# A two-layer transformer kernel: PSUM layout kept through the MLP, last MLP chunk computed plainly in token groups, adaLN dot products moved among the up projections

## The chip, the cores and the metric

The kernel runs on one core of one Trainium2 chip. The metric is device time in microseconds (us): the median of several executions. The engines are PE (TensorE, matrix multiplication), DVE (VectorE), ACT (ScalarE), POOL (GpSimd) and SP (SyncE, which here only issues transfers). PSUM, where PE leaves its products, has eight banks; a bank holds 512 fp32 values in each of 128 partitions.

## What is computed

Two layers over 512 latent tokens and 256 context tokens, model width 1024, MLP width 4096. Only the MLP and the modulation concern the change:

```python
def sq_relu_mlp(h, w1, w2):
    return jnp.square(jax.nn.relu(h @ w1)) @ w2
...
    for l in range(DEPTH):
        last = l == DEPTH - 1
        mod_x = (jax.nn.silu(c) @ w_ada[l] + b_ada[l])[:, None, :]
        mod_c = jax.nn.silu(c_ctx) @ w_ada[l] + b_ada[l]
...
        x = x + g1 * ox
        x = x + g2 * sq_relu_mlp(modulate(rmsnorm(x, norm_mlp[l]), sh2, sc2), w_ff1[l], w_ff2[l])
        if not last:
            h = h + cg1 * oc
            h = h + cg2 * sq_relu_mlp(modulate(rmsnorm(h, norm_mlp[l]), csh2, csc2), w_ff1[l], w_ff2[l])
    return rmsnorm(x, norm_final)
```

In layer 0 both streams go through the MLP (768 tokens, side by side as columns), in layer 1 only the latent one (512).

## The kernel before

Activations lie with features on partitions and tokens as columns. Every fp32 operand of a large product is split into a high and a low part (ACT copies the high part, L208; DVE subtracts it to get the low one, L217), and a product is three matmuls (`mm3`, all recorded on L200). Weights come in units by transfers from SP's queue (`load_unit`, L225 and L233) into four raw buffers, and are split in pieces of up to 512 columns, four pieces ahead of the task that needs them (`emit`, AP_ = 4). The work is a list of tasks. `merge` interleaves two lists by the costs written into the tasks; a scheduler then orders each engine's instructions, mostly in the order of the tasks, and later ones that are ready may go ahead.

The MLP (`layer_ff`) runs over chunks of the MLP width: 8 chunks in layer 0, 4 in layer 1. A chunk has an up projection (4 or 8 output tiles, one unit `w_ff1` each; relu and square on ACT, L1366 and L1367) and a down projection (2 or 4 blocks, one unit `w_ff2` each). The down projection multiplies 2 x 2 block matrices with seven products instead of eight: the tokens are cut into two halves (384 or 256 columns), the features into even and odd tiles. For this DVE forms sums of weight quarters (`quarter`, L244: S1 to S4) and of activations (`evac`: T1 to T4, L1357 and L1369), and what the seven products give is added in two ways. `gate` (L1418) adds a product times the modulation to the residual `x`; `keep` (L1357, in the first chunk a copy by ACT, L1426) adds it to one of three running sums U, 5, 7, which `finish` combines in the last chunk and passes through `gate`. Each product of the seven goes into a PSUM tile of one bank; `begin` opens a pool of eight such tiles for the MLP (`self.psum(0, 8)`), where the rest of the kernel has tiles of two banks (`A`) and of one bank (`B`).

In the last chunk the last two blocks (in layer 0 both) run five products first and then S1 and S4, with the norm of the first token half laid among these. `push` and `stat_push` (L514, L518) add the squares of `x` for the norm, `stat_end` sums them over partitions with a matmul (`ssum`), `rstd` (L528 to L532) makes the factor and `norm_h` (L545 to L549) the next input `h`. The norm of the second half follows everything. In layer 1 the final norm and the stores take the place of `norm_h` (`final_tasks`).

The output projection ahead of the MLP (`residual_tasks`, tiles `res`) ends in another form: its last four output tiles (TAIL0 = 4) run once for each of three token groups (0 to 255, 256 to 511, 512 to 767), and the norm of one group is laid among the products of the next.

The modulation vectors of layer 1 are dot products on DVE (`ada_rows_tasks`, L468): a task loads a piece of 128 rows by 512 columns of the transposed weight into one of three buffers (`rows`, N_RR = 3) and multiplies it with `silu(c)` and, for the first 32 of 96 tasks, also with `silu(c_ctx)`. Each is kept behind the last marked instruction of the MLP on DVE (`issue_after(self.mark.ins)`). In the emission they are merged among all tasks of layer 0's MLP but the first 4 and the last 40 (`ff[4:FT]`). Chunk 0's up projection also holds the adaLN work of layer 0 for two other vectors (`ff1`: 4 tasks of matmuls, 8 of double rows).

## Time and profile before

| | |
|---|---|
| median of 3 runs | 1646.73 us (1646.69 to 1647.88) |
| the profiled execution, its time | 1643.82 us |
| its span (first to last instruction) | 1642.0 us |
| MLP of layer 0, first matmul to the next layer's first | 418.4 to 992.5 us |
| MLP of layer 1, first matmul to the end | 1269.8 to 1642.0 us |

Times in the trace are microseconds from the span's start. PE is matmuls, PEld the loads of weights into the array, which overlap them. PEclk is the granted TensorE clock as a share of 2.4 GHz, a mean over the stretch. An idle time has what ended it behind "<-". A row "x120" of a timeline merges so many instructions that followed one another.

### The profile page before, as it was taken

How to read it: one execution, taken by the hardware profiler on the slowest of the kernel's cores; microseconds unless marked ns; L12 is line 12 of the kernel's file. 1: busy time of each engine (PE TensorE's matmuls, PEld its weight loads, DVE VectorE, ACT ScalarE, POOL GpSimd, SP SyncE). 2: the span in 40 equal slices, each digit the busy share in tenths (PEclk: the TensorE clock that was granted, in tenths of full speed). 3: DMA queues.
4: the chain of work that ended last, by engine and by line, in shares of the span. 5: the costliest groups of instructions: out<-in, count | busy, mean ns of one | idle time of the engine just before them, and what ended most of it. 6: DMA issues, size and time to landing. Idle time of an engine off the chain costs nothing.

```text
span 1642.0 us, 26299 instructions
## 1 busy us (share of the span) xinstructions
PE 1533.6 (93%) x9840; PEld 1375.8 (84%) x9840; DVE 1245.5 (76%) x2761; ACT 830.4 (51%) x1746; POOL 38.0 (2%) x78
## 2 busy tenths in 40 slices
PE   4999999998999999999999848999998999999995
PEld 2898567877799999999999737967887999999995
DVE  5665756877786988988979896677646785969688
ACT  4425467554445344344353334367754656464653
POOL 0010000000000000000000000101000000000000
PEclk8999999999899999999999968999999999999997
DMA  9352545553242413334345133524323232232311
GB/s 371 113 151 65 144 107 126 185 171 117 84 134 71 142 61 113 120 106 148 119 132 167 53 117 102 179 69 110 100 85 115 78 110 97 83 125 78 123 58 52
DMA packets 69103, 192.08 MB, mean 117 GB/s; under 512 B 8944, under 2 KB 11504, under 8 KB 68976
## 3 DMA queue, kind: packets, MB, share of 16 engines
q1 hardware_dynamic: 65584, 180.18, 34.1%
q0 software_dynamic: 2816, 9.70, 2.6%
q8 instruction: 77, 1.26, 0.3%
q10 hardware_dynamic: 576, 0.52, 0.1%
q14 instruction: 50, 0.41, 0.1%
HBM read 159.97 MB, written 10.49 MB: 104 GB/s over the span
## 4 chain that ended last, share of the span: by engine, by line
PE 76%; DVE 18%; ACT 2%; DMA 2%; issue 1%; SPq 0%; DVEq 0%; ACTq 0%
PE f L200 40%; PE A L200 10%; PE sc L200 4%; DVE x L1418 3%; PE oe L200 3%; DVE wt L217 3%; PE pv L200 3%; PE res L200 3%; DVE V L1357 3%; PE pT L1025 2%; PE rv L200 2%; DVE sum L244 2%; PE ada L200 2%; DVE rows L468 1%; PE ro L200 1%
## 5 line engine op out<-in xcount | busy, mean ns | idle before, releaser
L200 PEld LDWEIGHTS f<-h,wt 128*128 128x128 f32 x3120 | 451.6, 190 | 5.6 <-issue 3.8
L200 PE MATMUL f<-h,wt 128*128 128x256 f32 (+1 forms) x3120 | 454.1, 308 | 1.2 <-DVE nv L528 1.0
L200 PE MATMUL f<-act,wt 128*128 128x384 f32 (+1 forms) x2688 | 419.7, 316 | 19.7 <-DVE x L1418 10.4
L200 PEld LDWEIGHTS f<-act,wt 128*128 128x128 f32 x2688 | 401.6, 193 | 35.9 <-ACT wt L208 12.8
L217 DVE TENSOR_TENSOR wt<-raw,wt 128x512 fp32r<-128x512 f32 (+1 forms) x320 | 218.8, 689 | 88.1 <-ACT wt L208 85.6
L208 ACT ACTIVATE wt<-raw 128x512 fp32r<-128x512 f32 (+1 forms) x320 | 195.0, 626 | 165.4 <-PE f L200 64.0
L200 PE MATMUL A<-h,wt 128*128 128x512 f32 (+2 forms) x864 | 172.5, 358 | 1.8 <-DVE nv L528 1.3
L200 PEld LDWEIGHTS A<-h,wt 128*128 128x128 f32 x864 | 144.4, 192 | 28.3 <-DVE nv L528 2.4
L208 ACT ACTIVATE wt<-sum 128x512 fp32r<-128x512 f32 x128 | 77.5, 629 | 173.5 <-DVE sum L244 165.1
L1366 ACT ACTIVATE b<-f 128x384 f32<-128x384 f32 (+1 forms) x130 | 55.6, 430 | 125.2 <-PE f L200 125.2
L217 DVE TENSOR_TENSOR wt<-sum,wt 128x512 fp32r<-128x512 f32 x128 | 86.8, 689 | 12.0 <-ACT wt L208 10.7
L1418 DVE SCALAR_TENSOR_TENSOR x<-f,mod,x 128x256 f32<-128x256 f32 (+2 forms) x186 | 88.5, 501 | 1.4 <-PE f L200 1.0
L200 PE MATMUL sc<-k,q 96*128 96x512 f32 (+1 forms) x384 | 85.6, 350 | 2.6 <-ACT p L1007 2.0
L468 DVE SCALAR_TENSOR_TENSOR rows<-rows,sbc 128x512 f32<-128x512 f32 x128 | 86.5, 687 | 0.4
L208 ACT ACTIVATE act<-T 128x384 fp32r<-128x384 f32 (+1 forms) x128 | 58.9, 472 | 53.5 <-DVE T L1369 29.6
L200 PEld LDWEIGHTS sc<-k,q 96*128 96x128 f32 x384 | 62.8, 188 | 20.4 <-issue 5.5
L1357 DVE TENSOR_TENSOR V<-V,f 128x384 f32<-128x384 f32 (+1 forms) x162 | 79.3, 511 | 0.1
L217 DVE TENSOR_TENSOR act<-b,act 128x384 fp32r<-128x384 f32 (+1 forms) x96 | 46.8, 489 | 42.8 <-ACT act L208 42.7
L1006 DVE TENSOR_REDUCE st<-sc 128x1 f32<-128x768 f32 x64 | 60.7, 953 | 15.6 <-PE sc L200 15.2
L217 DVE TENSOR_TENSOR act<-T,act 128x384 fp32r<-128x384 f32 (+1 forms) x128 | 60.5, 487 | 12.4 <-ACT act L208 11.4
L1026 ACT ACTIVATE pT<-pT 128x384 f32<-128x384 f32 x128 | 56.5, 491 | 22.9 <-PE pT L1025 22.4
L200 PE MATMUL res<-mix,wt 128*128 128x256 f32 (+1 forms) x384 | 58.8, 312 | 2.3 <-DVE om L1046 1.9
(243 smaller groups left out, 1893.2 us busy)
## 6 DMA issues: line engine op xcount, KB each, us to landing
raw<-w_ff SPq DMA_DIRECT2D x128, 512.0 KB, 3.7
rows<-w_adaT SPq DMA_DIRECT2D x128, 256.0 KB, 2.8
raw<-w_in SPq DMA_DIRECT2D x22, 512.0 KB, 3.9
raw<-w_ada SPq DMA_DIRECT2D x16, 512.0 KB, 10.9
rows<-w_ada SPq DMA_DIRECT2D x32, 256.0 KB, 3.2
raw<-w_out SPq DMA_DIRECT2D x16, 512.0 KB, 3.6
x<-xd SPq DMA_DIRECT2D x6, 768.0 KB, 7.2
x<-xT SPq DMA_DIRECT2D x4, 768.0 KB, 6.8
```

What stands on the lines that cost most here:

```text
L200: self.nc.tensor.matmul(out, l, r, start=start, stop=stop)
L208: self.nc.scalar.activation(out, src, AF.Copy, **k)
L217: return self.nc.vector.tensor_tensor(out, src, hi.bitcast(F32), op=ALU.subtract)
L244: self.nc.vector.tensor_tensor(t, a, b, op=ALU.add)
L468: nc.vector.scalar_tensor_tensor(out, w, 1.0, self.sbc[:, v, half], op0=ALU.mult, op1=ALU.mult, accum_out=acc[:, v, i, j:j + 1])
L1006: nc.vector.tensor_reduce(st[:, 0:1], ps, axis=AX, op=ALU.max, negate=True)
L1025: nc.tensor.transpose(ps[:, kt, :], p[:, (k0 + kt) * P:(k0 + kt + 1) * P], self.ident)
L1026: nc.scalar.activation(s["pT", h, qt // 2][:, k0:k0 + 3, c], ps, AF.Copy)
L1357: add = lambda x, y, z, op=ALU.add: nc.vector.tensor_tensor(x, y, z, op=op)
L1366: nc.scalar.activation(b[:, at:at + n], ps, AF.Relu)
L1418: self.mark = nc.vector.scalar_tensor_tensor(x, ps[:, at - o:at - o + n], g[:, cond:cond + 1], x, op0=ALU.mult, op1=ALU.add)
```

## The change

`begin` no longer changes the PSUM pools: three tiles of two banks and two of one bank stay through the MLP. In layer 0 the two halves of an up tile, and the two output tiles of one of the seven products, share a two-bank tile; `keep` then handles both at once, 768 columns wide. In layer 1 `bank` hands out the two halves of such a tile one after the other, and an up tile is one product of 512 columns.

The last chunk is computed plainly, with eight products and neither sums of weights nor of activations (`split_plain`, `plain`). All blocks but the last take all tokens at once, the last one runs once for each token group, and the norm of a group is laid among the products of the next (`late`). `finish` moves into the last chunk's up projection, merged with its tasks. The norm's parts follow the token groups instead of the halves.

The dot products of layer 1's modulation are handed to `layer_ff`, which merges a share (14 of 96 tasks, at the end 13) into the up projection of each chunk but the last. In chunk 0 they follow the tasks of `ff1` in one list.

```diff
-            self.psum(0, 8)
...
+    def bank(self, name):
+
+        if self.half is None:
+            self.half = self.A(name, (P, 2, 512))
+            return self.half[:, 0, :]
+        t, self.half = self.half, None
+        return t[:, 1, :]
...
-        then = self.final_tasks(groups) if last else self.norm_tasks(l + 1, self.G1, 0, halves)
+        then = self.final_tasks(groups) if last else self.norm_tasks(l + 1, self.G1, 0, groups)
...
+        def split_plain(c, m, half):
...
+            f = act[c, m]
+            s = slice(0, w) if half is None else slice(half * hw, half * hw + hw)
+            b = st["b", m % 2][:, s]
+            self.hi(f[:, 0, s], b)
+            self.mark = self.lo(f[:, 1, s], b, f[:, 0, s])
...
         def up(c, m, u):
+            if last:
+                ps = self.bank("f1")
+                self.lin1(ps, u, H, NK, 0, w)
+                evac(c, m, None, [(ps, 0, w)])
+                return
+            ps = self.A("f1", (P, 2, 512))
...
-        def keep(c, j, name, ps):
-            v = st[name][j]
-            if c == 0 and (name, j) not in st:
-                st[name, j] = True
+        def keep(c, blk, name, ps):
+            v = st[name, "all"][:, MP * blk:MP * blk + MP]
+            if c == 0 and (name, blk) not in st:
+                st[name, blk] = True
                 nc.scalar.activation(v, ps, AF.Copy)
             else:
                 self.mark = add(v, v, ps)
...
-        def product(c, u, i, j, name, then=None):
+        def product(c, u, blk, name):
             q, f = use[name]
-            ps = self.B([P, hw], "f2")
+            ps = self.bank("f2")[:, None, :hw] if last else self.A("f2", (P, 2, 512))[:, :, :hw]
             t = u.pieces[name].t
-            for p in range(CP):
-                s = slice((i * CP + p) * P, (i * CP + p + 1) * P)
-                self.mm3(ps, t[:, 0, s], t[:, 1, s], *part(c, p, q), p == 0, p == CP - 1)
-            (then or f)(c, j, ps)
+            for i in range(MP):
+                for p in range(CP):
+                    s = slice((i * CP + p) * P, (i * CP + p + 1) * P)
+                    self.mm3(ps[:, i, :], t[:, 0, s], t[:, 1, s], *part(c, p, q), p == 0, p == CP - 1)
+            f(c, blk, ps)
...
+        def plain(c, u, blk, i, odd, gs):
+
+            ps = self.A("f2")
+            m = 2 * (MP * blk + i) + odd
+            for o, n, _ in gs:
+                for side, name in enumerate((A21, A22) if odd else (A11, A12)):
+                    t = u.pieces[name].t
+                    for p in range(CP):
+                        s = slice((i * CP + p) * P, (i * CP + p + 1) * P)
+                        f = act[c, 2 * p + side]
+                        self.mm3(ps[:, o:o + n], t[:, 0, s], t[:, 1, s], f[:, 0, o:o + n], f[:, 1, o:o + n],
+                                 side == p == 0, side == 1 and p == CP - 1)
+            for o, n, cond in gs:
+                self.gate_update(l, m, ps, 5, o, n, cond)
+                self.stat_push(m, o, n)
...
+        spread = self.extra.pop(("ff", l), [])
         for c in range(n_chunk):
...
+            if c == n_chunk - 1:
+                ups = merge(ups, [Task(1, lambda j=j: finish(j)) for j in range(4)])
+            extra = self.extra.pop(("ff1", l), []) if c == 0 else []
+            share = -(-len(spread) // max(n_chunk - 1 - c, 1))
+            extra, spread = extra + spread[:share], spread[share:]
+            out += merge(ups, extra)
             blocks = [Unit(a["w_ff2"][l, c * n_blk + blk], 2048, "st") for blk in range(n_blk)]
...
+            if c < n_chunk - 1:
+                for blk in range(n_blk):
+                    out += block(c, blk, blocks[blk])
+        out.append(Task(0, self.stat_start))
+        for blk in range(n_blk - 1):
+            out += plain_tasks(c, blocks[blk], blk, whole)
+        late = []
+        for i, g in enumerate(groups):
+            ts = plain_tasks(c, blocks[-1], n_blk - 1, [g])
+            for j, t in enumerate(ts):
+                out.append(t)
+                share = -(-len(late) // (len(ts) - j))
+                out += late[:share]
+                late = late[share:]
+            late = list(then[i])
+        return out + late
...
-            tasks += e.pop(("mid", l), []) + merge(ff[:4], e.pop(("ff1", l), [])) + merge(ff[4:FT], e.pop(("ff", l), [])) + ff[FT:]
+            tasks += ff
```

## Rows read from the trace of the kernel before

**Rows 1.** The page, part 1: busy us (share of the span) and instructions by engine

```profile
PE 1533.6 (93%) x9840; PEld 1375.8 (84%) x9840; DVE 1245.5 (76%) x2761; ACT 830.4 (51%) x1746; POOL 38.0 (2%) x78
```

**Rows 2.** Windows: stretch, length, busy us of PE, PEld, DVE, ACT, POOL, PEclk, DMA

```profile
418.40:460.30 41.90, 39.60 (x262) 36.16 (x261) 29.48 (x70) 19.75 (x46) 0.00 (x0) 0.97 0.33 108
...
524.40:557.00 32.60, 31.04 (x170) 28.82 (x169) 31.36 (x70) 11.54 (x21) 0.00 (x0) 1.00 0.29 96
557.00:590.20 33.20, 33.20 (x194) 33.20 (x193) 25.85 (x59) 15.93 (x31) 0.00 (x0) 1.00 0.32 105
...
851.80:883.70 31.90, 30.75 (x170) 28.89 (x170) 30.63 (x68) 11.54 (x21) 0.00 (x0) 1.00 0.40 123
...
917.00:950.00 33.00, 24.94 (x127) 24.01 (x126) 31.99 (x71) 8.55 (x17) 0.00 (x0) 0.84 0.19 65
...
971.50:992.50 21.00, 2.90 (x4) 1.18 (x4) 17.59 (x39) 9.18 (x19) 0.00 (x0) 0.55 0.52 189
...
1402.20:1442.00 39.80, 39.80 (x338) 39.80 (x337) 38.47 (x79) 18.89 (x35) 0.00 (x0) 1.00 0.34 109
```

**Rows 3.** PE timeline, layer 0's last down projection: start, us, engine, line, what, [idle before]

```profile
916.95 19.55 PE L200 MATMUL f<-act,wt 128*128 128x384 f32 x108
944.44 6.82 PE L200 MATMUL f<-act,wt 128*128 128x384 f32 x24 [7.94 <-DVE x L1418]
960.61 1.65 PE L200 MATMUL ssum<-ss,one 128*128 128x384 f32 x2 [9.35 <-DVE ss L518]
...
988.39 1.62 PE L200 MATMUL ssum<-ss,one 128*128 128x384 f32 x2 [17.08 <-DVE ss L518]
...
992.55 7.75 PE L200 MATMUL A<-h,wt 128*128 128x384 f32 x30 [1.26 <-DVE nv L528]
```

**Rows 4.** PE timeline, layer 0's output projection up to the MLP

```profile
368.31 24.09 PE L200 MATMUL res<-mix,wt 128*128 128x512 f32 x156 [0.93 <-DVE om L1046]
...
411.41 1.22 PE L200 MATMUL ssum<-ss,one 128*128 128x256 f32 x2 [6.25 <-DVE ss L518]
413.50 1.22 PE L200 MATMUL ssum<-sq,one 128*128 128x256 f32 x2 [0.87 <-ACT sq L514]
416.50 1.92 PE L200 MATMUL ada<-rows,sc 128*32 128x512 f32 x4 [1.78 <-DVE nv L528]
```

**Rows 5.** PE timeline, layer 1's MLP: an up projection, and its last down projection

```profile
1356.62 45.73 PE L200 MATMUL f<-h,wt 128*128 128x256 f32 x384
...
1573.07 15.82 PE L200 MATMUL f<-act,wt 128*128 128x256 f32 x132
...
1624.44 6.61 PE L200 MATMUL f<-act,wt 128*128 128x256 f32 x36
```

**Rows 6.** PE timeline, layer 1's input projection: 48 matmuls of 512 columns

```profile
1012.39 11.50 PE L200 MATMUL A<-h,wt 128*128 128x512 f32 x48 [0.43 <-ACT rx L698]
```

**Rows 7.** Groups by line and form: xcount | busy, mean ns of one | idle before

```profile
L217 DVE TENSOR_TENSOR wt<-sum,wt 128x512 fp32r<-128x512 f32 x128 | 86.8, 689 | 12.0 <-ACT wt L208 10.7
...
L1357 DVE TENSOR_TENSOR V<-V,f 128x384 f32<-128x384 f32 x112 | 59.1, 553 | 0.0
...
L531 DVE SCALAR_TENSOR_TENSOR nq<-nv,nq 128x768 f32<-128x768 f32 x5 | 4.8, 955 | 3.2 <-ACT nq L530 3.2
```

**Rows 8.** Windows of the dot products alone (L468): stretch, length, DVE busy, PEclk, DMA

```profile
524.40:557.00 32.60, 5.62 (x16) 1.00 0.29 96
557.00:590.20 33.20, 7.00 (x20) 1.00 0.32 105
```

**Rows 9.** DVE timeline, chunk 0's up projection: the fourth and fifth row in succession

```profile
450.76 0.68 DVE L468 SCALAR_TENSOR_TENSOR dot<-rows,sbc 128x512 f32<-128x512 f32 x1
...
453.48 0.69 DVE L468 SCALAR_TENSOR_TENSOR dot<-rows,sbc 128x512 f32<-128x512 f32 x1 [1.30 <-DMA rows<-w_adaT]
```

**Rows 10.** DVE timeline, chunk 1's down projection: the second gate of the first product

```profile
532.81 0.61 DVE L1418 SCALAR_TENSOR_TENSOR x<-f,mod,x 128x384 f32<-128x384 f32 x1
```

More of the change, by code (lines that the diff above doesn't have):

```diff
@@ L53 @@
 TAIL1 = 2
-FT = -40
 TL = False
@@ L158, in __init__ @@
         self.dp = pool("dp", N_DP)
-        self.ps = None
+        self.ps = self.half = None
         self.es = es
```

115 lines of the change are left out of this document (54 added, 61 removed).

## The prediction

> **What bounds the kernel now.** I read the page's busy times first, then the windows by stage, then the PE timeline of the stages that came out too long, then the DVE's work in them. Over the span PE is busy 93% and DVE 76% [rows 1], but the MLP of each layer has stretches with other limits [rows 2]. In layer 0 an up projection of one chunk (192 matmuls) takes 33.2 us with PE busy throughout, 173 to 174 ns a matmul. A down projection has 168 of them, so 29.3 us if nothing holds it; the six of chunks 1 to 6 (the first is 524.40 to 557.00, the last 851.80 to 883.70) take 192.8 us together, 32.1 each, and DVE is busy for 31 of those 32. So DVE holds PE for 2.8 us in each, 17 us in all. In the up projection the same DVE has 7 us to spare.
>
> The dear place is the last chunk of layer 0. Its down projection starts at 916.95 and the next layer's first matmul at 992.55 [rows 3]: 75.6 us for the same 168 matmuls. PE waits 7.94 us for a gate, 9.35 us for the sum of squares, 17.08 us for the second one; DVE is busy for 32.0 of 33.0 us at the start of it, and the granted clock sinks to 0.55 at the end [rows 2]. Layer 1 has the same ending, smaller: its last down projection runs from 1573.07 to 1631.05, 58.0 us [rows 5], where the others take 39.8 [rows 2]. Its other stages have no gap on PE at all.
>
> **Term 1, the last chunk of layer 0.** The seven products become eight plain ones: 4 output tiles over (512, 256) columns and 4 in three groups of 256, that is 48 matmuls of 512 and 144 of 256, with the norm of a group laid among the products of the next. The kernel has this very form already, at the end of the output projection of the same layer (residual_tasks with TAIL0 = 4: the same tiles, the same three groups, 12 matmuls a product, the same norm_tasks). So I take its time rather than add one up: from its first matmul at 368.31 to the moment PE is free for the next stage at 416.50 (the adaLN matmuls there have no counterpart) are 48.2 us, of which 6.25 + 0.87 + 1.78 are waits [rows 4]. 48.2 - 75.6 = **-27.4 us**. DVE has less to do than before: no weight sums, 4 split pieces a block in place of 7 (689 ns each [rows 7]), no activation sums, no dot products. The four `finish` steps move into the up projection of that chunk, which has no dot products any more; DVE was busy there for some 19 us without them (below), so they are hidden. Without that cover they would lie on the path with up to 16 us: 4 times 8 instructions of about 0.5 us each (an addition takes 0.55 [rows 7]). Bounds: -33, if the waits of 9 us go too, and -15, if half of the present waits stay.
>
> **Term 2, layer 1.** Its last down projection becomes 144 matmuls of 512 and 96 of 256. A matmul of 256 goes at 45.73 / 384 = 119.1 ns [rows 5]; one of 512 at 11.50 / 48 = 239.6 ns at most [rows 6]. 144 x 0.2396 + 96 x 0.1191 = 45.9 us in place of 58.0: **-12.1 us**. The two norms around it are as they were. The up projection turns 48 matmuls of 256 into 24 of 512 a tile: 238.2 against 239.6 ns or a little under it, so I take 0 (bounds +1 and -4 us over 720 pairs). In the other down projections DVE is busy 38.5 of 39.8 us [rows 2] and now has six banks in pairs rather than eight single ones to be late in: 0, with +5 as the bound. Bounds of the term: -17 and -6.
>
> **Term 3, chunks 0 to 6 of layer 0.** All 128 dot products of layer 1's adaLN leave the down projections; a share of 14 rows goes into each up projection. The first 32 rows carry two dot products each. Ten dot products took 7.00 us in one up projection [rows 8], 0.70 each, and without them DVE was busy for 25.85 - 7.00 = 18.9 us there [rows 2]. So:
> - Chunks 3 to 6: 18.9 + 14 x 0.70 = 28.7 us in 33.2: hidden. Chunk 2 (4 double rows): 31.5, just hidden.
> - Chunk 1: 18.9 + 28 x 0.70 = 38.5 in 33.2, 5 us too much. It also has the last rows behind the last tile, ahead of the first product's evacuation. +4 us after what its down projection loses now (3.3).
> - Chunk 0: it also keeps the 8 double rows and 4 matmul tasks that it has now. 29.5 [rows 2] + 19.6 = 49.1 us in a window of 41.9. 7 us too much, and the rows behind the first two tiles can't use the time in which DVE waits for them: +8 us (0 to 20).
>
> In the down projections DVE falls to 31.4 - 5.6 = 25.8 us [rows 2, 8], and a wide `keep` costs at most 955 ns where two narrow ones cost 1106 [rows 7], another 1 us a chunk. But the PSUM turns get shorter. The release of the first product's pair of banks is the gate that ends at 533.4, 9.0 us after the down projection began at 524.4 [rows 2, 10]. With eight single banks PE runs 8 products ahead (8 x 6 x 174 ns = 8.4 us); with three two-bank tiles it has three pairs, 6.3 us. The products ahead of that gate are the same afterwards (activation splits, then the last rows). So I expect a wait of 2.7 us in each, before the fourth pair, in place of 2.8 spread out: 0 for chunks 2 to 6. Behind it the unloaded DVE catches up. Term 3: **+12 us**, bounds -17 (all present waits go) and +25. The row loads go past nothing new: they stay in SP's queue among the weights, in front of which they wait for a dot product to free one of three buffers.
>
> **Sum.** -27.4 - 12.1 + 12 = -27.5 us. The profiled execution has a span of 1642.0 and a time of 1643.82; the median shown is 1646.73, 2.9 more. The span becomes 1614.5, the median about 1619.
>
> **Rivals.** (A) *The up projection swallows the dot products.* PE needs the late activations only from the third product on, and DVE had idle time in chunk 0. Then term 3 is about -15 and the time 1592. For it: DVE's total per chunk (18.9 + 25.8 + 9.8) is below PE's 62.5 us. Against it: the double rows lie in the first two chunks, where it isn't.
>
> (B) *Three PSUM tiles hold PE all through the down projections*, not once: a second wait like the first, 3 us in seven of them, 1640. The Trainium skill ("Perfetto Trace Analysis", Optimization Strategy) warns of just this: a gap that repeats on the engine that should be saturated can mean that there is no PSUM for the next tile, by buffer count or tile size. By that rule the change goes the wrong way. The rows of before show PE held in these stages even with eight banks, which agrees; they also show DVE full at the time, so which of the two it was they can't tell. Further, the skill ("TensorE: Matmul & The Clock Gate", A second HAM failure mode: psum-queue depth-cycling) reports a clock that oscillates when PE stops briefly between PSUM turns. In the rows of before the granted clock stayed at 1.00 in the down projections that lost 2.6 to 3.3 us, and fell to 0.84 and 0.55 only with waits of 8 to 17 us, so I give it nothing of its own.
>
> (C) *Slower: the rows are paced by their three buffers.* Place: the up projections of chunks 0 to 6. Dot products are in order on DVE, and one that waits for its row holds the splits of the next tile's activations and weights behind it. Behind three rows in a row the next came 2.72 us after the one before it, with 1.30 us of waiting for the transfer [rows 9]. At that pace 14 rows take 38.1 us, 4.8 too long, in six chunks 29 us, and chunk 0 with some 17 rows behind its first two tiles 46 us where there are about 22: +24. With terms 1 and 2 that is +13.5: 1660. It decides from 33.3 / 14 = 2.4 us a row on. Against it: three loads in flight make it about (3 + 1.4) / 3 = 1.5 us, and the rows come in threes with 8 us between.
>
> (D) *The tail doesn't become like the output projection's*: DVE comes late into it, and term 1 is -13: 1633. The change not doing what it says can't be seen in the code; every part has its place in the order.
>
> **Chances.** Forecast 0.60 (own range 1607 to 1631), A 0.15, B 0.09, C 0.07, D 0.09. A measurement of this kernel can tell about 0.2%, 3.3 us. Faster: the forecast, A, B, D but for their ends, 0.91; within: 0.03; slower: C, 0.06. The range leaves out most of C and the far half of A: 1594 to 1642.
>
> **What would show it.** After the change: from the start of layer 0's last down projection to the next layer's first matmul 48 us (over 60 is D); layer 1's last down projection 46 us; in chunk 0 a wait of some 8 us on PE around the first down projection for an activation split or a gate, in chunk 1 some 7; in chunks 2 to 6 one wait of 2 to 3 us before the fourth pair, with DVE as releaser (many of them is B, none is A); up projections of 33 us in which DVE waits little for rows (many waits for the row transfers are C). It would be wrong above all by how late DVE comes out of the first two up projections.

## The result, and the profile after

The changed kernel takes 1657.07 us (median of 4 runs, 1655.85 to 1657.78), the kernel before beside it 1646.82 us (1646.69 to 1647.88): a ratio of 1.006, interval 1.0043 to 1.0077. It is slower by 10 us where 28 us of gain were forecast. The spans of the profiled executions are 1655.8 and 1642.0 us.

PE is busier by 19 us although it executes 740 matmuls fewer than before ([rows 1] against part 1 of the page after):

```profile
PE 1552.9 (94%) x9100; PEld 1351.4 (82%) x9100; DVE 1183.5 (71%) x2564; ACT 802.4 (48%) x1635; POOL 38.2 (2%) x78
```

The plain last chunk works. These are PE rows of the changed kernel from layer 0's last down projection to the next layer's first matmul (the matmuls A); they answer [rows 3]. The columns are start, us, engine, line, operation, count and, in brackets, the idle time before the row with what ended it.

```profile
966.47 23.62 PE L206 MATMUL f<-act,wt 128*128 128x512 f32 x153
...
990.60 5.98 PE L206 MATMUL f<-act,wt 128*128 128x256 f32 x48
996.86 1.44 PE L206 MATMUL f<-act,wt 128*128 128x256 f32 x10 [0.28 <-DVE x L1243]
...
1009.03 1.22 PE L206 MATMUL ssum<-ss,one 128*128 128x256 f32 x2 [6.21 <-DVE ss L524]
1010.71 0.98 PE L206 MATMUL A<-h,wt 128*128 128x384 f32 x2 [0.46 <-ACT h L554]
```

From 966.47 (three matmuls of the projection stand earlier, at 961.44) to 1010.71 are 44.2 us, where 916.95 to 992.55 were 75.6. The waits of 7.94, 9.35 and 17.08 us have become one of 6.21 us, the one that the output projection's tail had before [rows 4].

The first chunks went the other way. Windows of chunks 0, 1 and 2 after (stretch, length, busy us of PE, PEld, DVE, ACT, POOL, PEclk, DMA share, GB/s), to be held against 72.7 us for chunk 0 before (418.4 to 491.1) and 65.8 for chunk 1 (to 556.9):

```profile
405.40:512.00 106.60, 86.49 (x437) 73.55 (x438) 85.95 (x214) 40.80 (x82) 0.00 (x0) 0.86 0.37 115
512.00:587.90 75.90, 68.02 (x362) 65.01 (x361) 63.51 (x145) 27.74 (x52) 0.00 (x0) 0.93 0.32 102
587.90:657.20 69.30, 64.48 (x362) 61.99 (x361) 56.42 (x123) 27.84 (x52) 0.00 (x0) 1.00 0.36 113
```

Chunk 0 starts 13 us earlier than before (405.39 in place of 418.43) and ends 21 us later. Among its PE rows stand these waits, and below them the ACT row that the longest one hangs on:

```profile
446.31 1.91 PE L206 MATMUL ada<-rows,sc 128*32 128x512 f32 x2 [2.33 <-DMA rows<-w_ada]
...
471.31 6.97 PE L206 MATMUL f<-h,wt 128*128 128x384 f32 x24 [7.03 <-ACT b L1409]
...
488.21 23.92 PE L206 MATMUL f<-act,wt 128*128 128x384 f32 x120 [3.42 <-ACT wt L214]
```

```profile
470.77 0.49 ACT L1409 ACTIVATE b<-f 128x384 f32<-128x384 f32 x1 [8.79 <-DVE dot L474]
```

PE waits 7.03 us for ACT to read an up tile; ACT, idle for 8.79 us, waits for a dot product. Why it must, the experiments show.

A middle chunk of layer 0 after, from 726.12 to the next at 794.46 (chunks 3 to 6 are alike, 68.3 to 68.9 us, where all but chunk 0 had 65 to 66 before). PE first:

```profile
726.12 29.60 PE L206 MATMUL f<-h,wt 128*128 128x384 f32 x168
755.55 2.07 PE L206 MATMUL f<-act,wt 128*128 128x384 f32 x11
757.46 4.32 PE L206 MATMUL f<-h,wt 128*128 128x384 f32 x24
761.62 4.50 PE L206 MATMUL f<-act,wt 128*128 128x384 f32 x25
769.91 24.72 PE L206 MATMUL f<-act,wt 128*128 128x384 f32 x132 [3.79 <-DVE x L1453]
```

Two things are new. The second half of the last up tile (x24) comes behind the first 11 matmuls of the down projection, and after 36 matmuls, which is three pairs of products, PE waits 3.79 us for the gate of the first pair. DVE before that gate (the wide `keep`, the last two dots of the chunk, the two gates):

```profile
762.00 0.95 DVE L1363 TENSOR_TENSOR V<-V,f 128x768 f32<-128x768 f32 x1 [2.27 <-PE f L206]
...
766.89 0.69 DVE L474 SCALAR_TENSOR_TENSOR rows<-rows,sbc 128x512 f32<-128x512 f32 x1
...
767.50 0.69 DVE L474 SCALAR_TENSOR_TENSOR rows<-rows,sbc 128x512 f32<-128x512 f32 x1
...
768.72 1.14 DVE L1453 SCALAR_TENSOR_TENSOR x<-f,mod,x 128x384 f32<-128x384 f32 x2
```

And the windows of the 8 us behind the wait show what it costs further: the granted clock is 0.62 and 0.52 in the first four us, and PE starts 15 matmuls there in place of the 27 of the next four.

```profile
769.90:771.90 2.00, 1.99 (x7) 2.00 (x8) 2.00 (x4) 0.00 (x0) 0.00 (x0) 0.62 0.61 223
771.90:773.90 2.00, 2.00 (x8) 2.00 (x8) 2.00 (x5) 0.00 (x0) 0.00 (x0) 0.52 0.52 104
773.90:775.90 2.00, 2.00 (x13) 2.00 (x12) 2.00 (x6) 1.15 (x2) 0.00 (x0) 1.00 0.43 166
775.90:777.90 2.00, 2.00 (x14) 2.00 (x13) 1.64 (x3) 0.00 (x0) 0.00 (x0) 1.00 0.00 0
```

Layer 1 after, PE rows around a down projection, and of the last one; they answer [rows 5]:

```profile
1504.59 1.11 PE L206 MATMUL f<-act,wt 128*128 128x256 f32 x8
1505.64 5.87 PE L206 MATMUL f<-h,wt 128*128 128x512 f32 x24
1511.35 3.58 PE L206 MATMUL f<-act,wt 128*128 128x256 f32 x28
1516.05 0.51 PE L206 MATMUL f<-act,wt 128*128 128x256 f32 x2 [1.12 <-ACT wt L214]
1516.99 35.82 PE L206 MATMUL f<-act,wt 128*128 128x256 f32 x286 [0.44 <-DVE wt L223]
...
1600.12 41.51 PE L206 MATMUL f<-act,wt 128*128 128x512 f32 x212
1642.14 3.16 PE L206 MATMUL f<-act,wt 128*128 128x256 f32 x24
```

The last down projection has become short (1600.12 to 1645.30, 45.2 us where it was 58.0), but the others, which had no gap before, now wait. In the one shown PE stops after 36 matmuls (8 and 28), three products of twelve. What ends the stop is ACT's split of a piece of weights, and not a gate; the first gate of this projection was over more than 3 us earlier (DVE row below). In the four us behind the stop the granted clock is 0.73 and 0.50 (windows below).

```profile
1512.37 0.48 DVE L1453 SCALAR_TENSOR_TENSOR x<-f,mod,x 128x256 f32<-128x256 f32 x1
```

```profile
1517.00:1519.00 2.00, 2.00 (x13) 2.00 (x14) 2.00 (x5) 0.87 (x2) 0.00 (x0) 0.73 0.66 227
1519.00:1521.00 2.00, 2.00 (x11) 2.00 (x11) 2.00 (x4) 0.82 (x2) 0.00 (x0) 0.50 0.57 172
```

Chunks 1 and 2 take 88.9 and 89.0 us where they took 85.4. Chunk 0 takes 96.6 in place of 86.8, but its up products begin 7.1 us earlier, 23.7 us after the output projection's first matmul in place of 30.9.

In all runs below the same two stages are measured: layer 0's from the output projection's first matmul to layer 1's first matmul, layer 1's from its output projection's first matmul to the end. The attention between them takes 246.0 to 247.7 us in all of them but the changed kernel (243.7). Stages are of one profiled execution each; e4, e9, e10 and e12 to e17 were timed once, the others in several rounds. Beside all these runs the kernel before took 1637.4 to 1647.9 us, so that a difference of a few us between times of single runs shows nothing by itself.

| kernel | time us | layer 0's stage | layer 1's stage |
|---|---|---|---|
| before | 1646.8 | 368.31 to 992.55: 624.2 | 1238.94 to 1642.0: 403.1 |
| after | 1657.1 | 368.14 to 1010.71: 642.6 | 1254.42 to 1655.8: 401.4 |
| e3, plain last chunk alone | 1603.4 | 366.00 to 961.58: 595.6 | 1208.52 to 1600.0: 391.5 |
| e2, and the new PSUM layout | 1637.3 | 367.39 to 988.56: 621.2 | 1235.15 to 1636.7: 401.6 |
| e1, or the dots' new place | 1618.4 | 366.21 to 975.16: 609.0 | 1222.32 to 1614.2: 391.9 |
| e4, after without layer 1's dots | 1609.9 | 365.85 to 961.18: 595.3 | 1208.08 to 1608.1: 400.0 |
| e9, e1 with six single tiles | 1624.6 | 366.03 to 986.02: 620.0 | 1232.51 to 1622.6: 390.1 |
| e10, after with four pairs | 1641.8 | 366.64 to 992.50: 625.9 | 1239.60 to 1640.1: 400.5 |
| e12, after, up halves single | 1640.2 | 368.91 to 996.01: 627.1 | 1241.99 to 1638.4: 396.4 |
| e15, after, both halves read late | 1637.8 | 367.97 to 997.10: 629.1 | 1244.81 to 1635.9: 391.1 |
| e14, e1 with three tiles in layer 1 | 1621.0 | 365.74 to 977.58: 611.8 | 1223.77 to 1619.2: 395.4 |
| e13, e1, chunk 0's rows not loaded | 1618.8 | 369.84 to 979.26: 609.4 | 1225.25 to 1616.7: 391.5 |
| e16, e9, dots with their own scratch | 1611.5 | 368.51 to 974.71: 606.2 | 1221.40 to 1609.7: 388.3 |
| e8, e1 with dots thinned | 1593.8 | 366.24 to 953.61: 587.4 | 1200.82 to 1593.0: 392.2 |
| e17, e8 and e16 together | 1595.6 | 366.50 to 958.97: 592.5 | 1205.27 to 1593.7: 388.4 |
| e11, e8, pairs through chunk 0's ups | 1596.6 | 366.99 to 959.33: 592.3 | 1205.63 to 1595.1: 389.5 |

### The profile page after: what moved, and what is told of

It reads as the page before. It is cut to its first block, busy times and chain, and to the rows that moved or that the text cites. A ratio compares the mean times of both kernels' runs of the same rounds, so it can differ in the third digit from the quotient of the medians.

```text
span 1655.8 us, 24510 instructions
## 1 busy us (share of the span) xinstructions
PE 1552.9 (94%) x9100; PEld 1351.4 (82%) x9100; DVE 1183.5 (71%) x2564; ACT 802.4 (48%) x1635; POOL 38.2 (2%) x78
## 3 DMA queue, kind: packets, MB, share of 16 engines
q1 hardware_dynamic: 65584, 180.18, 34.7%
## 4 chain that ended last, share of the span: by engine, by line
PE 84%; DVE 10%; DMA 3%; ACT 3%; issue 1%; SPq 0%; DVEq 0%; ACTq 0%
PE f L206 48%; PE A L206 10%; PE sc L206 4%; PE oe L206 3%; PE pv L206 3%; PE res L206 3%; PE rv L206 2%; PE pT L1031 2%; PE ada L206 2%; DVE act L223 1%; DVE rows L474 1%; PE ro L206 1%; DMA rows<-w_adaT 1%; PE q L206 1%; DVE dot L474 1%; DMA raw<-w_ada 1%
## 5 line engine op out<-in xcount | busy, mean ns | idle before, releaser
L206 PE MATMUL f<-h,wt 128*128 128x384 f32 (+2 forms) x2400 | 466.9, 355 | 10.3 <-ACT b L1409 7.7
L206 PE MATMUL f<-act,wt 128*128 128x256 f32 (+2 forms) x2664 | 436.1, 324 | 41.2 <-DVE x L1453 15.3
L206 PEld LDWEIGHTS f<-h,wt 128*128 128x128 f32 x2400 | 419.9, 191 | 54.3 <-ACT b L1409 14.2
L223 DVE TENSOR_TENSOR wt<-raw,wt 128x512 fp32r<-128x512 f32 x326 | 222.0, 687 | 150.5 <-ACT wt L214 148.1
L214 ACT ACTIVATE wt<-raw 128x512 fp32r<-128x512 f32 x326 | 201.4, 627 | 228.1 <-PE f L206 124.9
L206 PEld LDWEIGHTS A<-h,wt 128*128 128x128 f32 x864 | 143.0, 190 | 27.5 <-ACT h L554 2.8
L1409 ACT ACTIVATE b<-f 128x384 f32<-128x384 f32 (+2 forms) x98 | 50.5, 518 | 149.5 <-PE f L206 135.0
L206 PEld LDWEIGHTS sc<-k,q 96*128 96x128 f32 x384 | 62.8, 188 | 20.4 <-issue 5.5
L1363 DVE TENSOR_TENSOR V<-V,f 128x768 f32<-128x768 f32 (+1 forms) x86 | 62.5, 726 | 21.6 <-PE f L206 21.4
L1453 DVE SCALAR_TENSOR_TENSOR x<-f,mod,x 128x256 f32<-128x256 f32 (+2 forms) x148 | 68.9, 503 | 6.5 <-PE f L206 4.7
L223 DVE TENSOR_TENSOR act<-b,act 128x384 fp32r<-128x384 f32 (+2 forms) x94 | 47.5, 515 | 25.0 <-ACT act L214 24.9
L1013 ACT ACTIVATE p<-sc,st 128x768 f32<-128x768 f32 x64 | 57.8, 905 | 5.6 <-DVE st L1012 4.4
```

The lines of the kernel that those rows point to most:

```text
L206: self.nc.tensor.matmul(out, l, r, start=start, stop=stop)
L214: self.nc.scalar.activation(out, src, AF.Copy, **k)
L223: return self.nc.vector.tensor_tensor(out, src, hi.bitcast(F32), op=ALU.subtract)
L1013: nc.scalar.activation(p, ps, AF.Exp, bias=st[:, 0:1], accum_out=st[:, 1:2])
L1363: add = lambda x, y, z, op=ALU.add: nc.vector.tensor_tensor(x, y, z, op=op)
L1409: nc.scalar.activation(b[:, at:at + n], ps, AF.Relu)
```

## The experiments

**Which part costs.** Three runs undo the PSUM layout, the dots' place, or both; in the expectations theory P puts the loss on the PSUM pairs, theory D on the dots.

e1, single-bank tiles again:

```diff
         def begin():
+            self.psum(0, 8)
...
-            ps = self.A("f1", (P, 2, 512))
             for half in range(2):
                 o = half * hw
+                ps = self.B([P, hw], "f1")
...
-        def product(c, u, blk, name):
-            ps = self.bank("f2")[:, None, :hw] if last else self.A("f2", (P, 2, 512))[:, :, :hw]
+        def product(c, u, i, j, name):
+            ps = self.B([P, hw], "f2")
```

> The changed kernel with the PSUM layout of before in the MLP (eight tiles of one bank from the start of the MLP to the last down projection, one product a tile, narrow keep); dot products among the up projections and plain last chunk as changed. Theory P (PSUM turns: with three two-bank tiles PE waits before the fourth pair of each down projection): the 3.3 us lost in each of chunks 2 to 6 of layer 0, some 6 in chunks 0 and 1 and 3.5 in each of layer 1's three plain-free chunks come back, 1657 - 17 - 6 - 11 = 1623 us. Theory D (the dot products make DVE late out of the up projections, whatever the tiles): 1657, within 5 us, with the same waits at the same places.

e2, the dots merged among all tasks as before (`ff` without its last 45 tasks) and layer 0's own adaLN work (`ff1`) among the first four again, the pairs kept:

```diff
-            share = -(-len(spread) // max(n_chunk - 1 - c, 1))
-            extra, spread = extra + spread[:share], spread[share:]
-            out += merge(ups, extra)
+            out += ups
...
-            tasks += ff
+            tasks += merge(ff[:4], e.pop(("ff1", l), [])) + merge(ff[4:-45], e.pop(("ff", l), [])) + ff[-45:]
```

> The changed kernel with layer 1's dot products merged among all tasks of layer 0's MLP from the third up tile to the last down projection, as before; new PSUM layout and plain last chunk kept. Theory D: all 48 us that chunks 0 to 6 of layer 0 take longer come back, 1609 us. Theory P: chunks 0 and 1 come back (31 us), but with dot products in the down projections the wait for the three tiles in chunks 2 to 6 stays or grows to 4 to 6 us each, 1626 to 1640 us.

e3 is both edits.

> PSUM layout and place of the dot products both as before; only the plain last chunk in token groups (with finish in the up projection and the two-bank tiles from the last down projection on) and the up products of 512 columns in layer 1 remain. Both theories: the gains of the two last chunks alone, 1647 - 30 - 12 = 1605 us. If the gain of the last chunks hangs on the new layout: above 1620.

Measured: e1 1618.37 us (ratio to before 0.985, interval 0.983 to 0.9871), e2 1637.33 (0.9964, 0.9954 to 0.9975), e3 1603.39 (0.976, 0.9739 to 0.9782). With the changed kernel (1.006) they make a square of ratios: the pairs cost 0.020 with the old dots (0.9964 - 0.976) and 0.021 with the new ones (1.006 - 0.985), some 34 us of 1645; the dots' new place costs 0.009 with single tiles and 0.010 with pairs, some 15 us. By their times e1 and e2 suit P (1623, and 1626 to 1640), but neither theory holds alone: both parts lose, whatever the other does, and the plain last chunk alone gains 0.024, 39 us.

The dots' loss isn't spread evenly. With single tiles and the new place (e1), chunk 0 takes 95.2 us, chunk 1 69.4, but a middle chunk is PE from end to end:

```profile
644.84 33.44 PE L207 MATMUL f<-h,wt 128*128 128x384 f32 x192
678.12 29.64 PE L207 MATMUL f<-act,wt 128*128 128x384 f32 x168
```

That is 62.8 us from 644.84 to 707.60, and chunks 3 to 6 take 62.6 to 62.9, where the old place of the dots (e3) leaves 65.4 to 65.9. In the middle the dots' move gains 2.9 us a chunk, as meant; all of its price is in the first two chunks, 21.9 and 3.7 us over e3's.

e4 is the changed kernel without layer 1's dot products and row loads:

```diff
-                    for v in range(1 + two):
+                    for v in range(1 + two) if not l else ():
...
-                out.append(Task(1200 if two else 600, go, (unit,)))
+                out.append(Task(1200 if two else 600, go, () if l else (unit,)))
```

> The changed kernel without layer 1's dot products and their row loads (its modulation is left at the bias, so this part of the computation is missing). Theory P: chunks 0 and 1 come back, but the wait before the fourth pair stays at some 2.5 us in each down projection of layer 0 and layer 1 loses its 3.5 us a chunk as before: 1610 to 1618 us. Theory D: no wait is left in layer 0's down projections, 1605 us or less; layer 1 would then have to be explained otherwise.

Measured: 1609.86 us, just under what P expected. With the pairs and no dots at all, a wait before the fourth pair remains in chunks 1 to 6 of layer 0, 2.0 to 2.1 us each:

```profile
661.79 23.18 PE L206 MATMUL f<-act,wt 128*128 128x384 f32 x132 [2.12 <-DVE x L1455]
```

So the dots make 1.7 of the 3.8 us (the two ahead of the gate take 1.2, from 766.89 to 768.11), and the rest is there without any; layer 1's stage, which no dot touches, stays at 400.0 us.

**How the pairs cost.** Fewer banks (six in place of eight), or two things in one tile? In the expectations N is the number of banks, G the sharing.

e9 is e1 with `self.psum(0, 6)`; e10 is the changed kernel with four pairs from chunk 1 to the last up projection:

```diff
             m0, ups = 0, []
+            if c == 1:
+                out.append(Task(0, lambda: self.psum(4, 0)))
...
-        out.append(Task(0, self.stat_start))
+        out.append(Task(0, lambda: (self.psum(3, 2), self.stat_start())))
```

> As the run with eight single-bank tiles and the dots as changed (1618.4 us), but with six single tiles: the same six banks for up and down products as the three pairs have, yet one half or one product to a tile. If the pairs cost because PE can run only six banks ahead (theory N), the waits come back: chunks 3 to 6 of layer 0 at 66 to 69 us instead of 62.7, layer 1's chunks at 88 instead of 85.3, 1640 to 1657 in all. If they cost because two halves or two products share one tile and are freed and read as one (theory G): chunks at 62.6 to 63.5, layer 1's at 85.3, 1618 to 1625.

> The changed kernel with four two-bank tiles instead of three (and no single ones) from chunk 1's up products until the last chunk's down products, in both layers; chunk 0 as changed. Theory N (banks in flight): the wait of 3.8 us before the fourth pair goes, chunks 2 to 6 of layer 0 at 63 to 65.5 us instead of 68.3 to 69.4, layer 1's chunks 1 and 2 at 85.3 instead of 89: 1625 to 1640 in all. Theory G (two to a tile): the chunks stay at 66.5 to 69, layer 1's at 88 to 89: 1650 to 1658.

Measured: e9 1624.55 us, as G had it, e10 1641.84, just above N's range. Six single tiles bring a wait back in layer 0 (first row below, one of chunks 3 to 6, 1.6 to 1.8 us each, chunks 64.7 to 65.3), but none in layer 1 (second row: a whole down projection in one piece):

```profile
754.35 23.45 PE L207 MATMUL f<-act,wt 128*128 128x384 f32 x132 [1.61 <-DVE x L1456]
...
1393.93 40.23 PE L207 MATMUL f<-act,wt 128*128 128x256 f32 x336
```

Four pairs end at about the same wait in layer 0 (1.8 to 1.9 us, chunks 3 to 6 at 64.8 to 65.1). In layer 1 chunks 1 and 2 fall to 86.2 and 87.5 us, between the two theories, but the stage as a whole hardly does (400.5 against 401.4 us). So neither N nor G is right as put. The number of banks costs 11 us in layer 0 (620.0 against 609.0) and nothing in layer 1; the rest of the pairs' price, 642.6 - 620.0 = 22.6 us in layer 0 and all of the 10 in layer 1, is left for two things in one tile.

**What sharing does.** Three more runs. e12 takes the up halves out of the pairs, into the two single-bank tiles (the first two up tiles stay in pairs):

```diff
-            ps = self.A("f1", (P, 2, 512))
             for half in range(2):
                 o = half * hw
+                ps = self.B([P, hw], "f1")
```

> The changed kernel, its three pairs kept for the down products, but each half of an up tile (and each up tile of layer 1) in one of the two single-bank tiles beside them; the first two up tiles stay in pairs. If the two halves of an up tile cost because they share a tile, so that the second half waits for ScalarE's read of the first and the down products come between (theory H): layer 1's chunks 1 and 2 at 85.3 us instead of 89, chunks 2 to 6 of layer 0 at 66 to 67.5 with only the wait before the fourth pair left, and chunk 0 without its 7.0 us wait for ScalarE, 1630 to 1643 in all. If the price lies in the down products' pairs (theory D2): layer 1's chunks at 88 to 89, layer 0's at 68 to 69, 1650 to 1660.

e15 keeps the pairs, but reads neither half before both are computed; `pair` holds the first reader back until the second product of a tile is done:

```diff
                     self.mm3(ps[:, half, :hw], u[:, 0, s], u[:, 1, s], H(k)[:, 0, o:o + hw], H(k)[:, 1, o:o + hw], k == 0, k == NK - 1)
-                evac(c, m, half, [(ps[:, half, :hw], o, hw)])
+            for half in range(2):
+                evac(c, m, half, [(ps[:, half, :hw], half * hw, hw)])
...
-            f(c, blk, ps)
+            pair(lambda: f(c, blk, ps))
```

> The changed kernel with its pairs and its dots as they are, only that both halves of a pair are computed before either is read: the up tiles of layer 0, and the up tiles and products of layer 1 two by two (layer 0's products are read so already). Theory C: nothing of a tile is then waited for in the middle of it: layer 1's chunks 1 and 2 at 85.3 to 87 us instead of 89, chunk 0 of layer 0 without the 7.0 us wait for ScalarE, chunks 2 to 6 at 66.5 to 68.5 with the wait before the fourth pair left: 1632 to 1647 in all. If the pairs cost by their size alone: 1650 to 1658.

e14 is e1 with `self.psum(0, 3)` from layer 1's chunk 1 on.

> As the run with eight single-bank tiles and the dots as changed (1618.4 us), but from chunk 1 of layer 1 on with three single tiles for its up and down products. Theory C: where two halves share a tile and the second half's matmuls wait for the read of the first, three pairs let PE run only three products ahead in layer 1, so three singles must cost the same: chunks 1 and 2 of layer 1 at 87.5 to 89 us instead of 85.3, 1623 to 1630 in all. If three products ahead are enough and the pairs cost in another way: chunks at 85.3 to 86, 1617 to 1620.

Measured: e12 1640.19 us, e15 1637.82, e14 1621.04. Layer 1's stage falls to 391.1 us in e15, about that of the single tiles (391.9): once neither half is read before both are computed, the 10 us that the stage had lost are back. Chunk by chunk it is less than that. Chunks 1 and 2 take 87.2 and 86.9 us, against 88.9 and 89.0 in the changed kernel and 85.3 with single tiles, so half of their price remains; the stage comes out even because e15 keeps the early start of layer 1 (23.8 us after the output projection's first matmul, where e1 has 30.9).

What is left of the wait ends as in the changed kernel, with ACT's split of a piece of weights. First e15, then e12:

```profile
1492.43 6.34 PE L206 MATMUL f<-act,wt 128*128 128x256 f32 x48
1499.45 0.51 PE L206 MATMUL f<-act,wt 128*128 128x256 f32 x2 [0.68 <-ACT wt L214]
```

```profile
1405.79 3.15 PE L206 MATMUL f<-act,wt 128*128 128x256 f32 x24
1411.04 35.90 PE L206 MATMUL f<-act,wt 128*128 128x256 f32 x300 [2.10 <-ACT wt L214]
```

PE has done two products of twelve when it comes to that piece in e12, three in the changed kernel and four in e15, and waits 2.10, 1.12 and 0.68 us for it; with single tiles (e1, e9) it doesn't wait at all. This suits the order in which halves wait for each other's reader: the fewer products PE can take meanwhile, the sooner it stands before weights that aren't split yet. Which products it passes over was not traced.

Three single tiles (e14) wait after 36 matmuls too, but for a gate:

```profile
1387.60 4.38 PE L207 MATMUL f<-act,wt 128*128 128x256 f32 x36
1393.25 10.50 PE L207 MATMUL f<-act,wt 128*128 128x256 f32 x84 [1.26 <-DVE x L1456]
```

They give chunks of 87.1 and 87.0 us (their ups start at 1342.54, 1429.63 and 1516.63), short of the 87.5 to 89 expected and above the rival's 85.3 to 86: half of the difference. Three open products thus cost something of this size, but the changed kernel's stop ends otherwise, so e14 doesn't show that its pairs cost in this way. e12's time lies where its theory H had it (1630 to 1643), its chunks between the theories: layer 1's stage is half way (396.4), with only the up tiles apart and the products still sharing, and in layer 0 chunks 3 to 6 take 66.7 to 68.2 us with one wait of 2.65 to 2.79 us each.

In layer 0, e15 takes 7 us from chunk 0 (99.5) and 4.6 from chunk 1 (71.3), and nothing from the middle chunks (chunks 3 to 6 at 68.0 to 68.8, where 66.5 to 68.5 was expected): the order of the up halves is restored there, yet the wait before the fourth pair is as long as in the changed kernel.

```profile
747.51 6.41 PE L206 MATMUL f<-act,wt 128*128 128x384 f32 x36
757.68 24.72 PE L206 MATMUL f<-act,wt 128*128 128x384 f32 x132 [3.76 <-DVE x L1462]
```

Against e9's 1.61 us at the same 36 matmuls, 2.1 us of this wait belong to the pair. DVE's rows of the two runs say of what: a single bank is free after one narrow `keep` and one gate, the pair only after the wide `keep` (0.95 us for 0.55) and both gates (0.5 more); the rest is that in e15 DVE begins on the last up tile 0.6 us later, behind ACT's late read, and has one more activation split (0.5) ahead of the gates. No run takes these apart.

**Why chunk 0 pays for the dots.** In the expectations, L stands for the rows' loads, V for a full DVE. e13 is e1, with the 14 rows of chunk 0 not loaded; the dots read values on chip, and the unused products of both dots of a row go to a scratch tile, where e1 writes those of the second over the row:

```diff
-                    w = unit.raw[:, 0:512]
+                    w = self.sbc[:, 0, half] if idle else unit.raw[:, 0:512]
...
-                        out = self.tmp("dot")[:, 0:512] if v < two else w
+                        out = self.tmp("dot")[:, 0:512] if v < two or idle else w
...
-                out.append(Task(1200 if two else 600, go, (unit,)))
+                out.append(Task(1200 if two else 600, go, () if idle else (unit,)))
```

> As the run with eight single-bank tiles and the dots as changed (1618.4 us), but the 28 dots of layer 1 that stand in chunk 0 of layer 0 read values already on chip, scaled to zero, instead of their 14 rows, which are not loaded: the first columns of layer 1's modulation are their bias alone. The dots' place and time on VectorE stay. If chunk 0's price comes from the row loads ahead of layer 0's own w_ada rows on their queue (theory L): chunk 0 at 75 to 85 us instead of 95.2, 1598 to 1610. If it comes from VectorE, full of dots when the first up tiles' sums are due (theory V): chunk 0 at 88 to 95, 1611 to 1619.

Measured: 1618.8 us, layer 0's stage 609.4 against 609.0, chunk 0 93.2 us against 95.2. Leaving out the loads gains next to nothing; even PE's wait for layer 0's own rows is still there (4.31 us in place of 4.48). But e13 takes twice as many scratch tiles for chunk 0's dots of layer 1, and the next run shows these tiles to be dear: a gain without the loads may be hidden by that. Its time fits V, but the ACT row shown above (8.79 us behind a dot) suggested a third cause. The first dot product of a two-dot row writes its unused products to a scratch tile, from the ring of seven out of which the up projection takes the tile `b` for ACT's read; the single dots write over their own row. Only the first 32 rows, those of chunks 0 to 2, are double. e16 is e9 with another place for these products, a PSUM bank of their own:

```diff
-                        out = self.tmp("dot")[:, 0:512] if v < two else w
+                        out = w if v >= two else self.tmp("dot")[:, 0:512] if self.junk is None else self.junk
```

> As the run with six single-bank tiles (1624.6 us), but the first dot product of each two-dot row writes its (unused) products to a bank of PSUM of its own, and no longer to the ring of seven scratch tiles from which the up projection takes the tile for its ScalarE read. Theory S: in chunk 0 ScalarE's read of an up tile stands 8.8 to 9.1 us behind the dots because these hold the ring's tiles; then that wait goes, chunk 0 falls from about 96 us to 80 to 88, chunk 1 from 71 to 66 to 68, and the time to 1605 to 1617. Theory V: VectorE is simply full of dots, and the sums that the down products need come no sooner: 1619 to 1626.

Measured: 1611.47 us, 13 us below e9, within the range of theory S. ACT's reads in chunk 0 no longer wait for DVE but for the matmuls that fill the tile. First e9, then e16:

```profile
473.51 0.87 ACT L1411 ACTIVATE b<-f 128x384 f32<-128x384 f32 x2 [8.82 <-DVE dot L475]
```

```profile
461.49 0.49 ACT L1415 ACTIVATE b<-f 128x384 f32<-128x384 f32 x1 [1.96 <-PE f L208]
```

Chunk 0 falls to 84.7 us (417.31 to 501.98; e9 has 93.4, 415.46 to 508.89) and chunk 1 from 71.1 to 68.1. So the shared scratch ring cost nearly what the dots' new place loses on the whole, but in chunk 0 it is less than half: 8.8 us of the 20 that e9 has over e3's 73.3. What is left there, 84.7 against 73.3, was not taken apart. Two things stand in e16's rows: DVE is busy for 34.7 of the 36.6 us from 465.4 to 502.0, with dots in front of the first gates, and PE still waits 3.79 us for layer 0's own rows (`rows<-w_ada`), which go through the same three buffers as layer 1's; in e8, with no dots of layer 1 in chunk 0, it doesn't wait for them.

**A version that beats both.** e8 is e1 with the 128 dots thinned over chunks 1 to 6 by their number, none in chunk 0:

```diff
-            share = -(-len(spread) // max(n_chunk - 1 - c, 1))
-            extra, spread = extra + spread[:share], spread[share:]
+            left = sum(t.cost for t in spread) / max(n_chunk - 1 - c, 1) if c else 0
+            while spread and left > 0 and c < n_chunk - 1:
+                left -= spread[0].cost
+                extra, spread = extra + spread[:1], spread[1:]
```

> The changed kernel with eight single-bank tiles for the MLP again (one product and one half of an up tile each), its plain last chunk and its columns of 512 in layer 1 kept, and the dot products among the up products of chunks 1 to 6 only, 21 or 22 dots to a chunk by count, none in chunk 0. If the price of the dots' new place lies only in the first two chunks, where their two-dot rows and layer 0's own modulation meet the first up tiles: chunk 0 as with both undone (73 us), chunks 1 to 6 at 62.7 to 64 each instead of 65.5, 1586 to 1592 in all. If the dots cost wherever they are as dense as in chunk 1 (69.4 us there), the gain of 2.7 a chunk is lost again: 1600 to 1625.

e11 is e8 with the pairs kept through chunk 0's up products (`self.psum(0, 8)` only before its down products), e17 is e8 with e16's scratch and six tiles.

> The single tiles with the dots thinned over chunks 1 to 6, but chunk 0's up products still in the three two-bank tiles kept from the output projection, so that they may start before the last norm sum; eight single tiles from chunk 0's down products on. If the early start of 13 us in layer 0 and 7 us in layer 1 is worth something when chunk 0 has no dots of the next layer: 3 to 12 us below the run with single tiles from the start. If it is given back inside chunk 0, because the up products then wait for ScalarE's read of the other half of their tile and for the rows of the modulation: within 3 us of it.

> The same scratch bank with the dots thinned over chunks 1 to 6 (as in the run of 1593.8 us, which has eight banks and the shared ring). Theory S: ScalarE's waits of 2.1 us behind dots in chunks 1 and 2 go, these chunks fall to 64 to 65 us; the two banks fewer cost up to 1.8 us a chunk from the gate of the first product: 1592 to 1600. Theory V: chunks 1 and 2 stay at 66 and 64 or, with the banks' price, 66 to 68: 1598 to 1605.

Measured: e8 1593.79 us (0.9708, 0.9679 to 0.9737), e11 1596.63 (0.9724, 0.9702 to 0.9745), e17 1595.58. e8 lies 1.8 us above its expected range: chunk 0 is 72.3 us, but chunks 1 and 6 keep a wait of 1.83 us each and take 66.1 and 64.9. e11's early start buys nothing in layer 0: the up products begin 12 us earlier (404.25 against 416.54), yet chunk 0 ends at 493.10, after e8's 488.88. In layer 1 they begin 7.2 us earlier, and the stage is 2.7 us shorter (389.5 against 392.2). In e17 chunks 1 and 2 are 64.7 and 64.8 us and the waits behind dots are gone, but two banks fewer bring 1.7 to 2.4 us before the seventh product of every chunk. These three can hardly be told apart; e8 is the fastest measured, 2.9% below the kernel before.

## Why the prediction was wrong

Its sum was -27.5 us; the spans differ by +13.8. What failed is term 3, put at +12, and within term 2 the 0 for layer 1's other down projections. By its terms:

**Term 1, the last chunk of layer 0: right.** -27.4 was put for the down projection to the next layer's first matmul; the whole last chunk, its up projection included, went from 108.9 us (883.67 to 992.55) to 79.0 (931.68 to 1010.71), -29.9. Taking the price from the same form elsewhere in the kernel [rows 4] held. (The prediction's count of the plain products is wrong, 144 matmuls of 256 columns where the trace has 192; the time wasn't added up from it.) The four `finish` steps cost nothing in the up projection, as forecast.

**Term 2, layer 1: right in the part that was costed.** -12.1 was put for the last down projection; from the last up projection to the end it is 103.1 us (1552.65 to 1655.8) in place of 114.5 (1527.50 to 1642.0), -11.4. The up products in 512 columns take 45.1 us for 192 (e1 and e8), 235 ns each, against 45.7 for 384 of 256 [rows 5]: the 0 was right to 0.6 us a chunk. The step that failed is the sentence behind it: "0, with +5 as the bound" for the other down projections. Layer 1's stage gained 1.7 us in all, so its other parts lost some 10 (403.1 - 11.4 = 391.7, and it is 401.4): chunk 0 lost 9.8, chunks 1 and 2 together 7.0, and the early start gave 7.1 back. I counted six banks in pairs as six products ahead. The halves of a pair wait for each other's reader, and PE stands after three products before weights that aren't split yet; with both halves read late (e15) the stage is 10.3 us shorter.

**Term 3, chunks 0 to 6 of layer 0: wrong, +12 forecast, +48 measured, beyond its bound of +25.** Step by step, from the end of each chunk against the output projection's start:

- Chunk 0, +8 forecast, +21 measured: it ended 122.8 us after the output projection's first matmul before, 143.8 after. The count of DVE's work (49 us in a window of 42) could not see that the dots also hold the scratch tile that ACT needs to read the up tiles (e16: 9 us less, of the 23 that e1's chunk 0 has over e8's), nor the chained up halves (e15: 7 us), nor that PE would wait for layer 0's own rows (2.43 and 2.33 us).
- Chunk 1, +4 forecast, +10.1 measured (75.9 against 65.8), for the first two of these reasons: 3.0 for the ring (e16), 4.6 for the halves (e15).
- Chunks 2 to 6, 0 forecast, +17.0 measured (343.8 us against 326.8). In chunks 3 to 6 the mechanism was the one forecast, a single wait before the fourth pair with the gates of the first as its end (chunk 2 has several short ones instead), and its size was under-put, 2.7 us against 3.8. That the pair needs both its gates had been counted [rows 10]; what was wrong is when they come. The prediction let the gates keep their old place, 9.0 us after the down projection's start. In the changed kernel both stand together behind activation sums, splits and two dots, 5.8 us after their `keep` (762.95 to 768.72); in e15, where nothing comes between the first 36 matmuls, PE goes on 10.2 us after the start (747.51 to 757.68). Left out altogether was that the wait is paid a second time in the clock behind it: 132 matmuls took 24.72 us, while in two chunks of e9 with a granted clock of 1.00 they took 23.43 and 23.45, 1.3 us less. 62.8 us without any wait (e1) + 3.8 + 1.3 = 67.9 of the 68.3.

**The rivals.** A was half seen: with single tiles the middle up projections do swallow the dots (e1), but no kernel with the pairs did. B named the right resource and the wrong price: it put one more wait of 3 us per chunk, in the down projections; the pairs cost some 34 us in all. The Trainium skill ("Perfetto Trace Analysis", Optimization Strategy) names buffer count and tile size for a gap that repeats on the engine that should be saturated; the runs agree as to the count, 11 us for six tiles in place of eight, and two things to a tile cost 22.6 more, both in layer 0. C, which gave nearly the right time (1660), has little in the rows to bear it out: the first dots of the two-dot rows of chunks 0 and 1 wait for their rows 4 times, 4.3 us in all, and later dots twice, 1.4 us, where C had six chunks losing 4.8 us each and chunk 0 24; and with the loads of chunk 0 left out (e13) the time stays, with the reservation made there. That it was near is luck. D didn't happen.

**The clock.** I gave the short waits no clock price, since stretches with 2.6 to 3.3 us lost in small pieces had kept 1.00 [rows 2]. In one piece, 3.79 us are followed by four us at 0.62 and 0.52, that is mostly at the lower of its two levels (1.2 and 2.4 GHz). In layer 1 a stop of 1.12 and 0.44 us with two matmuls in between is followed by 0.73 and 0.50. The Trainium skill ("TensorE: Matmul & The Clock Gate", A second HAM failure mode: psum-queue depth-cycling) tells of throughput lost to the clock after brief stops between PSUM turns; the trace here agrees, at 1.3 us for each wait of 3.79 us.

**The early start** was not foreseen: since the pool is not changed, the first up products no longer wait for the norm's last PSUM tiles and begin at 405.39 in place of 418.43. In layer 0 nothing of it is left at the end of chunk 0; e11, where only chunk 0's up products keep the pairs, shows the same. In layer 1 7.1 us are gained at the start and 9.8 lost in chunk 0.

What stays open: half of layer 1's price (1.8 of the 3.7 us a chunk remain when both halves are read late), which order of PE's products leads to the wait for weights there, and what remains of chunk 0's loss with the scratch ring freed.

## What to carry to other kernels

Count the PSUM tiles that are truly independent, not the banks: when a reader takes one half of a shared tile before the other half is computed, the pair is worth less than two open products; computing both halves first cost no bank and gave layer 1's stage its 10 us back. Before work is moved beside other work, list every buffer ring that its instructions draw from, the scratch outputs nobody reads included: the ring shared with the evacuation cost 13 us here. Price one wait of 3 to 4 us on PE higher than the same time in small pieces, and change such things one at a time: here one of three parts gained 39 us and the other two gave back 49.

## What the runs showed of the hardware

- A wait of 3.79 us on PE is followed by a granted clock of 0.62 and 0.52 over four us and then 1.00; PE waits of 1.61 and 1.73 us in two chunks of e9 leave it at 1.00 over the whole chunk. In between it goes either way: of six waits of 2.01 to 2.12 us in e4, two are followed by 132 matmuls in 24.71 and 24.72 us (a granted clock of 0.64 and 0.65 over the first four us) and four by 132 in 23.18 or 23.19 us; of two waits of 1.83 us in e8, one is followed by 120 matmuls in 22.64 us and the other in 21.42.
- A matmul of 512 columns takes 235 ns in a long row (45.14 us for 192), 2 x 119 ns being the price of the same columns in two.
- A double-wide addition on DVE (`keep`, 128 x 768 fp32 from PSUM) takes 0.95 us against 2 x 0.55 for two narrow ones [rows 7].
